# Other places in SBUF, modulo 512 bytes, for the operands of the float32r products of a two-layer hybrid transformer kernel

## The chip, the cores and the metric

One core of a Trainium2 chip runs the whole forward pass as one program. The metric is the device time of one execution in microseconds; the time before is the median of 3 runs.

## What is computed

Two layers over 256 tokens of width 2048, all in float32. Layer 0 mixes with HGRN2 (8 heads, chunked recurrence) and MLA attention (8 heads, low-rank queries and keys, rotary parts), layer 1 with retention (8 heads, keys of 256, values of 512). Behind each mixer stands a gated feed-forward part with a short causal convolution, then a gated embedding.

```python
h = x
for i in range(DEPTH):
    u = rmsnorm(h, norm_mix[i])
    h = h + (even_mixer(u, ...) if i % 2 == 0 else odd_mixer(u, ...))
    h = h + conv_ffn(rmsnorm(h, norm_ffn[i]), ffn_w_gate[i], ffn_w_up[i], ...)
    gate = jax.nn.sigmoid(rmsnorm(h, norm_ple[i]) @ ple_w_gate[i])
    h = h + (p[i] @ ple_w_proj[i]) * gate
```

Nearly all of the work is products of the 256 tokens with weight matrices; some 520 MB of weights are read once.

## The kernel before, in words

**Split products.** A float32 weight block `raw` (128 partitions by up to 1024 columns, one DMA) is split into two float32r parts: `wh`, a rounding copy by ScalarE (L158), and `wl = raw - wh` by VectorE (L161). The activations are split in the same way: a tile `xs` of 128 partitions by 512 columns holds the high part of 256 tokens in its first half and the low part in its second. A product then is high by high, high by low and low by high; low by low is left out. For each matmul TensorE loads a 128 by 128 operand (the stationary one) and streams the other past it (the moving one).

**The feature-major product** (`gemm_fm`, L172 to 199) is most of the kernel. The weights are stationary, the tile `xs` is moving. A block of 1024 weight columns makes 8 matmuls of high weights with all 512 columns of `xs` (L184). After each second block (`RUN = 2`) the low weights of both follow, with the first 256 columns of `xs` (L186). So a high run of 16 matmuls and a low run of 16 alternate; where the number of blocks is odd there are runs of 8, and with `px` of 4. The same function is used with `xs`, `hs` (the feed-forward part), `xo` (retention), `xa`, `xb` (heads of layer 0) and `px` as the moving tile. `gemm_fm1` (L201 to 215) is the same for narrower outputs: L209, L211 and L212, each with 256 columns.

**The token-major product** (`gemm_tm`, L217 to 235; `first_values`, L238 to 288, for the first matrix) turns it round: 128 columns of `xs` are stationary, 512 columns of weights are moving, in the order high by high weights (L228, L263), high by low weights (L229, L264), low by high weights (L230, L265).

**Where the tiles lie.** Tile pools lie one behind another in each partition's memory, and the tiles in a pool likewise, so each tile's size sets the start of those behind it. The sizes above are multiples of 512 bytes, so every buffer of a tag has the same start modulo 512. `LOW_SHIFT = 320` puts a pad of 320 bytes ahead of `wl`; `shift(low, "low", 64)` and `shift(l1, "l1", 64)` put 64 bytes ahead of two stage pools. As the program lays them out, before the change: `xs`, `xa`, `xb`, `hs`, `xo`, `px`, `x_kva`, `x_qa`, `raw` and `wh` begin at 64 modulo 512, `wl` at 384. In layer 1's retention the tiles `rz`, `rat` and `rv` begin at 64. Each 128-column piece of a weight tile is 512 bytes, so the piece that a matmul uses doesn't change the place modulo 512, and the same goes for the column pieces of `xs`.

**The lead.** For a matmul, call the lead the place of the next matmul's stationary operand minus the place of its own moving operand, modulo 512. Before: 0 in a high run (64 - 64), 320 in a low run (384 - 64), and in the token-major product 0, 192, 0 in turn (64 - 64, 64 - 384, 64 - 64). Retention's L1008 (`rat` stationary, `rv` moving) has 0 throughout.

**Smaller things that the change touches.** `rope_tables` loads the positions into a tile `posi` of its own and copies it to `posf` (L420 to 423). `q_rope` (L804 to 816) scales `y` (tag `ly`, two buffers) into a second tile `lyg` (L810) and rotates that: TensorE multiplies it by a permutation (L772), GpSimd multiplies it in place (L773, by the helper at L302), VectorE combines (L774, L775).

Of the kernel before, what the change touches and what calls it, by code (L numbers as in the profile page):

```python
# [8 lines left out]
F32 = mybir.dt.float32  # L9
F32R = mybir.dt.float32r  # L10
BF16 = mybir.dt.bfloat16
I32 = mybir.dt.int32
AF = mybir.ActivationFunctionType
# [4 lines left out]
P = 128  # L18
T = 256
# [5 lines left out]
F_HALVES = ((0, 24), (24, 44))  # L25
KB = 4
RUN = 2
LOW_SHIFT = 320
EPS = 1e-6

HG_HEADS = 8
# [47 lines left out]
def hybrid_kernel(ctx, tc, io):  # L79
    nc = tc.nc  # L80
# [4 lines left out]
    xpool = ctx.enter_context(tc.tile_pool(name="xpool", bufs=NX, reuse_waits="tile"))  # L85
    wpool = ctx.enter_context(tc.tile_pool(name="wpool", bufs=4))
# [18 lines left out]
    def vcol(name, i=0, n=1):  # L105
        if name == "mix0":
            return vec0[:, i:i + n]
        a = VEC[name][0] + i
        return vec[:, a:a + n]
# [7 lines left out]
    def pump():  # L117
        for g in active[:]:
            if next(g, active) is active:
                active.remove(g)  # L120
# [17 lines left out]

    shifted = set()

    def shift(pool, name, n):


        if name not in shifted:
            shifted.add(name)
            pool.tile([P, n // 4], F32, name=f"pad_{name}", bufs=1)

    def load_w(src, width):
        return split_w(fetch_w(src, width), width)

    def fetch_w(src, width):
        raw = wpool.tile([P, width], F32, tag="raw", name="raw", bufs=4)
        nc.sync.dma_start(out=raw, in_=src)
        return raw

    def split_w(raw, width):
        wh = wpool.tile([P, width], F32R, tag="wh", name="wh", bufs=3)
        nc.scalar.copy(wh, raw)  # L158
        shift(wpool, "wl", LOW_SHIFT)
        wl = wpool.tile([P, width], F32R, tag="wl", name="wl", bufs=RUN + 2)  # L160
        nc.vector.tensor_tensor(wl, raw, wh.bitcast(F32), op=ALU.subtract)  # L161
        return wh, wl

    def blocks_of(blocks, n, width, kb, sub=None):

        sub = sub or kb
        for k0 in range(0, n, sub):
            k1 = min(n, k0 + sub)
            o = (k0 % kb) * width
            yield range(k0, k1), load_w(blocks[k0 // kb][:, o:o + (k1 - k0) * width], (k1 - k0) * width)  # L170

    def gemm_fm(blocks, xs):  # L172

# [43 lines left out]
    def gemm_tm(blocks, xs, sub=None):  # L217

        ps = [psum.tile([P, 512], F32, tag="mm", name="mm", bufs=5) for _ in range(2)]
        n = len(xs)  # L220
        for ks, (wh, wl) in blocks_of(blocks, n, 512, 2, sub):
            for kc in ks:
                x = xs[kc]
                o = (kc - ks[0]) * 512
                for m in range(2):
                    xh = x[:, m * P:(m + 1) * P]
                    xl = x[:, T + m * P:T + (m + 1) * P]
                    nc.tensor.matmul(ps[m], xh, wh[:, o:o + 512], start=(kc == 0), stop=False)  # L228
                    nc.tensor.matmul(ps[m], xh, wl[:, o:o + 512], start=False, stop=False)  # L229
                    nc.tensor.matmul(ps[m], xl, wh[:, o:o + 512], start=False, stop=(kc == n - 1))  # L230
            if ks[-1] % 4 == 3:
                pump()
        return ps

    def first_values(src, xs):


        ps = [[psum.tile([P, 512], F32, tag="mm", name="mm", bufs=5) for _ in range(2)] for _ in range(2)]  # L238
        n = len(xs)
        with tc.tile_pool(name="first", bufs=4) as first:  # L240
            raws = {}

            def fetch(kc):
                if kc < 2:
                    for g in range(2):
                        raws[kc, g] = first.tile([P, 512], F32, tag="raw0", name="raw0")
                        nc.sync.dma_start(out=raws[kc, g], in_=src[kc][:, g * 512:(g + 1) * 512])
                elif kc < n:
                    raws[kc] = fetch_w(src[kc], 1024)

            def split_half(raw):
                wh = first.tile([P, 512], F32R, tag="wh0", name="wh0")
                nc.scalar.copy(wh, raw)
                wl = first.tile([P, 512], F32R, tag="wl0", name="wl0")
                nc.vector.tensor_tensor(wl, raw, wh.bitcast(F32), op=ALU.subtract)
                return wh, wl

            def products(kc, g, wh, wl, o):
                x = xs[kc]
                for m in range(2):  # L260
                    xh = x[:, m * P:(m + 1) * P]
                    xl = x[:, T + m * P:T + (m + 1) * P]
                    nc.tensor.matmul(ps[g][m], xh, wh[:, o:o + 512], start=(kc == 0), stop=False)  # L263
                    nc.tensor.matmul(ps[g][m], xh, wl[:, o:o + 512], start=False, stop=False)  # L264
                    nc.tensor.matmul(ps[g][m], xl, wh[:, o:o + 512], start=False, stop=(kc == n - 1))  # L265

            xs.fetch(0, 0)
            fetch(0)
            xs.fetch(0, 1)
            fetch(1)  # L270
            for i in range(1, 3):
                xs.fetch(i)
                fetch(2 * i)
                fetch(2 * i + 1)
            xs.fetch(3)
            for kc in range(n):
                if kc < 2:
                    for g in range(2):
                        products(kc, g, *split_half(raws[kc, g]), 0)
                else:  # L280
                    wh, wl = split_w(raws[kc], 1024)
                    for g in range(2):
                        products(kc, g, wh, wl, g * 512)
                    fetch(kc + 4)
                    if kc % 2 == 0 and kc // 2 + 3 < n // 2:
                        xs.fetch(kc // 2 + 3)
                if kc % 4 == 3:
                    pump()
        return ps
# [126 lines left out]
    rope_t = {}  # L416

    def rope_tables(tpool):
        posi = tpool.tile([P, T], I32, tag="posi", name="posi", bufs=1)
        nc.sync.dma_start(out=posi, in_=io["positions"])  # L420
        yield from steps(2)
        posf = tpool.tile([P, T], F32, tag="posf", name="posf", bufs=1)
        nc.vector.tensor_copy(posf, posi)
        for name in ("mla", "ret"):
            ang = tpool.tile([P, T], F32, tag="ang", name="ang", bufs=1)
            nc.vector.tensor_scalar(ang, posf, vcol(f"invf_{name}"), None, op0=ALU.mult)
            cs = cpool.tile([P, T], F32, name=f"cos_{name}")
            sn = cpool.tile([P, T], F32, name=f"sin_{name}")
            sin_of(sn, ang, 0.0, tpool)
            sin_of(cs, ang, 0.25, tpool)  # L430
            rope_t[name] = (cs, sn)
            yield


    def ffn_and_ple(i, st):
        rs = token_stats(st[0], D, 2)
        xs = st[1]
        cw, cb = f"cw{i}", f"cb{i}"
        st = new_norm()
        with tc.tile_pool(name=f"ffn{i}", bufs=2, reuse_waits="tile") as fp:  # L440
            silu = {}

            def gate(ps, f):
# [46 lines left out]
            xs = st[1]  # L490
# [174 lines left out]
    def even_mixer(rs, xs):  # L665
# [1 line left out]
        mix_a, mix_b = {}, {}  # L667
        first = first_values(io["w_hv"], xs)
        with tc.tile_pool(name="low", bufs=2) as low:
            shift(low, "low", 64)  # L670
            kpe = low.tile([P, 1, T], F32, name="kpe", bufs=1)
            with tc.tile_pool(name="l0a", bufs=2) as pool:
                hvs = {}
# [91 lines left out]
    def mla(pool, kpe, ckv, cq, rkv, rqa, mix, fill):  # L765
# [3 lines left out]
        def rotate(dst, y):  # L769
            ps = small([P, 2, T], "sm_rot")  # L770
            n = y.shape[1]
            nc.tensor.matmul(ps[:, 0:n], mcol("swap"), y, start=True, stop=True)  # L772
            mul(y, y, bcast(cos, n), nc.gpsimd)  # L773
            mul(dst, ps[:, 0:n], bcast(sin, n))  # L774
            nc.vector.tensor_tensor(dst, dst, y, op=ALU.add)  # L775
# [25 lines left out]
        qr, sqr, mv, pairs = {}, {}, {}, {}  # L801

        def q_rope(ps, g):
            yield from until(rqa, "bc")  # L804
            y = pool.tile([P, 2, T], F32, tag="ly", name="ly")
            mul(y, ps, bcast(rqa["bc"]))
            sq = pool.tile([P, 2, T], F32, name=f"sqr{g}", bufs=1)
            nc.scalar.activation(sq, y, AF.Square)
            yg = pool.tile([P, 2, T], F32, tag="lyg", name="lyg", bufs=1)
            nc.scalar.activation(yg, y, AF.Copy, scale=vcol("qr"))  # L810
            yield
            z = pool.tile([P, 2, T], F32, name=f"qr{g}", bufs=1)
            rotate(z, yg)
            for j in range(2):
                sqr[2 * g + j] = sq[:, j]
                qr[2 * g + j] = z[:, j]
# [111 lines left out]
    def odd_mixer(st):  # L928
        rs = token_stats(st[0], D, 2)
        xs = st[1]  # L930
        st = new_norm()
        cs, sn = rope_t["ret"]
        with tc.tile_pool(name="l1", bufs=1, reuse_waits="tile") as l1, \
                tc.tile_pool(name="l1t", bufs=2, reuse_waits="tile") as lt:
            shift(l1, "l1", 64)
            mx = {}
            rot = {}
            gates = {}
# [146 lines left out]
    xs = Arriving()  # L1085
# [120 lines left out]
```

## Time and profile before

| what | value |
|---|---|
| median of 3 runs | 2848.39 us (2848.35 to 2848.42) |
| the profiled execution's own time | 2848.95 us |
| its span, first to last instruction | 2847.1 us |
| busy: TensorE matmuls, weight loads | 2838.5 us, 2474.0 us |
| busy: VectorE, ScalarE, GpSimd | 1898.6 us, 1403.0 us, 84.7 us |
| granted TensorE clock | 1.000 of full speed |
| HBM over the span | 184 GB/s |

Read it so: matmuls are pipelined, and a matmul's recorded time (some 390 ns for 512 columns) is longer than the distance from its start to the start of the next. What the stream costs is that distance, its pace. It is read from the chain of work that ended last: a piece of that chain is a row with a start, a length and a count of matmuls, and length by count is the pace.

### The profile page before, as it was taken

To read this page: it belongs to the slowest core of one execution; us is meant where nothing else is said; L and a number is where in the kernel's file an instruction comes from. 1 tells how busy PE (TensorE), PEld (TensorE's weight loads), DVE (VectorE), ACT (ScalarE), POOL (GpSimd) and SP (SyncE) were. 2 spreads that over 40 slices of the span, in tenths; PEclk is the share of its full clock that TensorE was granted. 3 is DMA by queue.
4 is the path that set the end of the run, shared out by engine and by line. 5 is a ranking of instruction groups with operands and counts; after the bars stand their busy time and mean duration, and the time that the engine had idled before them with its cause. 6 is when DMAs were issued, how large, how long until landed. Compare 5 with 4: busy or idle time off the path is not lost.

```text
span 2847.1 us, 41083 instructions
## 1 busy us (share of the span) xinstructions
PE 2838.5 (100%) x16025; PEld 2474.0 (87%) x16025; DVE 1898.6 (67%) x2753; ACT 1403.0 (49%) x1844; POOL 84.7 (3%) x123
## 2 busy tenths in 40 slices
PE   9999999999999999999999999999999999999999
PEld 7888888888888888888888888888888888888888
DVE  8776787766557776785555555556777755777666
ACT  6665555444344444564444444445444433444444
POOL 1110300000000000000000000000000000000000
PEclk9999999999999999999999999999999999999999
DMA  7555445556655665565555555555665655666564
GB/s 242 175 157 163 133 154 189 188 191 192 192 187 191 189 189 188 187 194 183 182 180 182 189 185 181 178 178 185 196 191 186 193 189 189 192 188 194 186 194 165
DMA packets 147939, 525.58 MB, mean 185 GB/s; under 512 B 16544, under 2 KB 18336, under 8 KB 147744
## 3 DMA queue, kind: packets, MB, share of 16 engines
q1 hardware_dynamic: 147600, 522.95, 57.5%
q8 instruction: 125, 2.05, 0.3%
q14 instruction: 70, 0.57, 0.1%
q10 hardware_dynamic: 144, 0.01, 0.0%
HBM read 520.80 MB, written 2.10 MB: 184 GB/s over the span
## 4 chain that ended last, share of the span: by engine, by line
PE 98%; DVE 1%; DMA 0%; POOL 0%; issue 0%; ACT 0%; SPq 0%; DVEq 0%
PE mm L184 52%; PE mm L186 27%; PE mm L230 4%; PE mm L229 4%; PE mm L228 4%; PE sm_ro L1008 1%; PE mm L209 1%; PE mm L212 1%; PE mm L211 1%; PE mm L264 0%; PE mm L265 0%; PE sm_ra L987 0%; PE mm L263 0%; DMA raw<-in_w_hv 0%; PE sm_sc L875 0%; DVE wl L161 0%
## 5 line engine op out<-in xcount | busy, mean ns | idle before, releaser
L161 DVE TENSOR_TENSOR wl<-raw,wh 128x1024 fp32r<-128x1024 f32 (+1 forms) x990 | 1200.4, 1219 | 819.3 <-ACT wh L158 801.6
L158 ACT CAST wh<-raw 128x1024 fp32r<-128x1024 f32 (+1 forms) x990 | 1032.0, 1043 | 1205.2 <-PE mm L184 776.7
L184 PE MATMUL mm<-xs,wh 128*128 128x512 f32 x4288 | 1028.8, 391 | 0.0
L184 PEld LDWEIGHTS mm<-xs,wh 128*128 128x128 f32 x4288 | 787.1, 188 | 153.1 <-DVE xs L311 0.4
L186 PEld LDWEIGHTS mm<-xs,wl 128*128 128x128 f32 x4288 | 541.2, 189 | 19.1
L186 PE MATMUL mm<-xs,wl 128*128 128x256 f32 x4288 | 550.5, 281 | 0.0
L184 PE MATMUL mm<-hs,wh 128*128 128x512 f32 x1408 | 337.2, 391 | 0.0
L184 PEld LDWEIGHTS mm<-hs,wh 128*128 128x128 f32 x1408 | 258.2, 188 | 49.6
L229 PE MATMUL mm<-wl,xs 128*128 128x512 f32 x512 | 202.0, 394 | 0.0
L230 PE MATMUL mm<-wh,xs 128*128 128x512 f32 x512 | 201.8, 394 | 0.0
L228 PE MATMUL mm<-wh,xs 128*128 128x512 f32 x512 | 201.7, 394 | 0.0
L186 PEld LDWEIGHTS mm<-hs,wl 128*128 128x128 f32 x1408 | 179.4, 189 | 7.3
L186 PE MATMUL mm<-hs,wl 128*128 128x256 f32 x1408 | 181.7, 281 | 0.0
L295 ACT COPY evt<-mm 128x256 f32<-128x256 f32 x300 | 98.2, 374 | 92.9 <-PE mm L186 92.9
L184 PE MATMUL mm<-xo,wh 128*128 128x512 f32 x512 | 122.7, 391 | 0.0
L230 PEld LDWEIGHTS mm<-wh,xs 128*128 128x128 f32 x512 | 96.2, 188 | 22.4
L229 PEld LDWEIGHTS mm<-wl,xs 128*128 128x128 f32 x512 | 96.1, 188 | 22.1
L228 PEld LDWEIGHTS mm<-wh,xs 128*128 128x128 f32 x512 | 96.2, 188 | 21.9
L184 PEld LDWEIGHTS mm<-xo,wh 128*128 128x128 f32 x512 | 94.0, 188 | 18.5 <-DVE xo L1025 0.3
L399 DVE TENSOR_TENSOR h<-h,mm 128x256 f32<-128x256 f32 x128 | 48.1, 415 | 35.7 <-PE mm L186 35.7
L186 PEld LDWEIGHTS mm<-xo,wl 128*128 128x128 f32 x512 | 64.9, 189 | 2.4
L186 PE MATMUL mm<-xo,wl 128*128 128x256 f32 x512 | 65.9, 281 | 0.0
(275 smaller groups left out, 1952.5 us busy)
## 6 DMA issues: line engine op xcount, KB each, us to landing
raw<-in_wg SPq DMA_DIRECT2D x176, 512.0 KB, 3.7
raw<-in_wu SPq DMA_DIRECT2D x176, 512.0 KB, 4.1
raw<-in_wd SPq DMA_DIRECT2D x176, 512.0 KB, 3.9
raw<-in_w_oqk SPq DMA_DIRECT2D x64, 512.0 KB, 4.2
raw<-in_w_ov SPq DMA_DIRECT2D x64, 512.0 KB, 3.7
raw<-in_w_og SPq DMA_DIRECT2D x64, 512.0 KB, 3.5
raw<-in_w_oo SPq DMA_DIRECT2D x64, 512.0 KB, 4.1
raw<-in_wpg SPq DMA_DIRECT2D x60, 512.0 KB, 3.6
```

The costliest lines, as they stand in the source:

```text
L158: nc.scalar.copy(wh, raw)
L161: nc.vector.tensor_tensor(wl, raw, wh.bitcast(F32), op=ALU.subtract)
L184: nc.tensor.matmul(ps[j], w[:, o:o + P], xs[kc], start=(kc == 0), stop=False)
L186: nc.tensor.matmul(ps[j][:, 0:T], w[:, o:o + P], xs[kc][:, 0:T], start=False, stop=(kc == n - 1))
L209: nc.tensor.matmul(ps[:, j], w, x[:, 0:T], start=(kc == 0 and j == 0), stop=False, skip_group_check=True)
L211: nc.tensor.matmul(ps[:, j], w, x[:, T:2 * T], start=False, stop=False, skip_group_check=True)
L212: nc.tensor.matmul(ps[:, j], wl[:, o:o + P], x[:, 0:T], start=False, stop=(kc == n - 1 and j == ncol - 1), skip_group_check=True)
L228: nc.tensor.matmul(ps[m], xh, wh[:, o:o + 512], start=(kc == 0), stop=False)
L229: nc.tensor.matmul(ps[m], xh, wl[:, o:o + 512], start=False, stop=False)
L230: nc.tensor.matmul(ps[m], xl, wh[:, o:o + 512], start=False, stop=(kc == n - 1))
L295: nc.scalar.copy(tmp[:, j], ps[j][:, T:2 * T])
L399: nc.vector.tensor_tensor(h[i][:, j], h[i][:, j], ps[j][:, 0:T], op=ALU.add)
```

## The change

It moves tiles, and shares or drops two small ones to make room. The pads are now kept in one table. `xs` gets 192 bytes ahead of it and so begins at 256 modulo 512; `wh` gets 128 more and begins at 384; the buffers of `wl` are 512 bytes longer than their contents, begin at 384, and the contents stand at their start in the token-major product (384) and 192 bytes further in the feature-major one (64). The pads of the stage pools are set so that `hs`, `px`, `x_kva`, `x_qa`, `xo`, `rz`, `rat` and `rv` also begin at 256. The leads become 128 in a high run (384 - 256), 320 in a low run as before (64 - 256), and 384 throughout the token-major product (256 - 384); L1008 stays at 0. No matmul, load, copy or DMA of the products is added or left out. `posi` takes the buffer of `ang`, and `q_rope` scales `y` in place, so that `lyg` is gone.

```diff
-LOW_SHIFT = 320
+LOW_AT = {"features": 48, "tokens": 0}
+PADS = {"xs": 192, "wh": 128, "low": 256, "ret": 256, "ffn": 192}
...
-    def shift(pool, name, n):
-        if name not in shifted:
+    def shift(pool, name):
+        if name not in shifted and PADS[name[:3]]:
             shifted.add(name)
-            pool.tile([P, n // 4], F32, name=f"pad_{name}", bufs=1)
+            pool.tile([P, PADS[name[:3]] // 4], F32, name=f"pad_{name}", bufs=1)
+    shift(xpool, "xs")
...
-    def split_w(raw, width):
+    def split_w(raw, width, form):
+        shift(wpool, "wh")
         wh = wpool.tile([P, width], F32R, tag="wh", name="wh", bufs=3)
         nc.scalar.copy(wh, raw)
-        shift(wpool, "wl", LOW_SHIFT)
-        wl = wpool.tile([P, width], F32R, tag="wl", name="wl", bufs=RUN + 2)
+        wl = wpool.tile([P, 1024 + 128], F32R, tag="wl", name="wl", bufs=RUN + 2)
+        wl = wl[:, LOW_AT[form]:LOW_AT[form] + width]
         nc.vector.tensor_tensor(wl, raw, wh.bitcast(F32), op=ALU.subtract)
...
-        posi = tpool.tile([P, T], I32, tag="posi", name="posi", bufs=1)
+        posi = tpool.tile([P, T], I32, tag="ang", name="posi", bufs=1)
...
         with tc.tile_pool(name=f"ffn{i}", bufs=2, reuse_waits="tile") as fp:
+            shift(fp, f"ffn{i}")
...
-            shift(low, "low", 64)
+            shift(low, "low")
...
-            yg = pool.tile([P, 2, T], F32, tag="lyg", name="lyg", bufs=1)
-            nc.scalar.activation(yg, y, AF.Copy, scale=vcol("qr"))
+            nc.scalar.activation(y, y, AF.Copy, scale=vcol("qr"))
             yield
             z = pool.tile([P, 2, T], F32, name=f"qr{g}", bufs=1)
-            rotate(z, yg)
+            rotate(z, y)
...
-            shift(l1, "l1", 64)
+            shift(l1, "ret")
```

The rest of the diff hands `form` ("features" or "tokens") down to `split_w`; `gemm_tm` and `first_values` say "tokens".

## Rows read from the trace of the kernel before

**Rows 1.** The page: busy time, share of the span and instructions of each engine; then the chain that ended last, by engine; and from the view of that chain, its shares by line.

```profile
PE 2838.5 (100%) x16025; PEld 2474.0 (87%) x16025; DVE 1898.6 (67%) x2753; ACT 1403.0 (49%) x1844; POOL 84.7 (3%) x123
...
PE 98%; DVE 1%; DMA 0%; POOL 0%; issue 0%; ACT 0%; SPq 0%; DVEq 0%
...
by line: PE mm L184 52.2%; PE mm L186 26.9%; PE mm L230 4.3%; PE mm L229 4.3%; PE mm L228 4.3%; PE sm_ro L1008 0.6%; PE mm L209 0.6%; PE mm L212 0.5%; PE mm L211 0.5%; PE mm L264 0.4%; PE mm L265 0.4%; PE sm_ra L987 0.4%; PE mm L263 0.4%; D
```

**Rows 2.** The view of line L184, matmuls alone: moving and stationary tile, count, duration in ns (least, median, greatest), first and last start in us. L186 has the same counts.

```profile
L184 PE MATMUL mm<-xs,wh x4288: 387/389/501, 63.7 to 2827.5; 128*128 128x512 f32 x195
...
L184 PE MATMUL mm<-hs,wh x1408: 388/389/398, 696.5 to 2740.3; 128*128 128x512 f32 x176
...
L184 PE MATMUL mm<-xo,wh x512: 387/389/499, 1569.8 to 2007.3; 128*128 128x512 f32 x171
...
L184 PE MATMUL mm<-xa,wh x128: 387/393/499, 262.8 to 380.8; 128*128 128x512 f32 x128
...
L184 PE MATMUL mm<-xb,wh x128: 387/389/481, 383.2 to 427.5; 128*128 128x512 f32 x128
...
L184 PE MATMUL mm<-px,wh x64: 389/392/398, 1161.9 to 2830.3; 128*128 128x512 f32 x64
```

**Rows 3.** The view of line L228, matmuls alone, columns as in rows 2; L229 and L230 have the same counts.

```profile
L228 PE MATMUL mm<-wh,xs x512: 387/395/398, 1285.9 to 1917.0; 128*128 128x512 f32 x171
...
L228 PE MATMUL mm<-wh,x_kva x16: 387/395/398, 274.8 to 326.0; 128*128 128x512 f32 x16
```

**Rows 4.** The chain that ended last in a long stretch of token-major products (layer 1's values and gates), the first and the last of its 149 pieces of one matmul each, in the order L228, L229, L230: start in us, length in us, what.

```profile
1293.49 0.23 PE mm L230
...
1327.84 0.23 PE mm L228
```

**Rows 5.** The timeline between 449.9 and 458.3 us, where a high run ends and a low run begins: start us, length us, engine, line, what; the loads of a run and its matmuls are rows of their own.

```profile
449.68 1.29 PE L184 MATMUL mm<-xs,wh 128*128 128x512 f32 x5
...
450.59 2.06 PEld L186 LDWEIGHTS mm<-xs,wl 128*128 128x128 f32 x16
450.81 2.05 PE L186 MATMUL mm<-xs,wl 128*128 128x256 f32 x16
```

**Rows 6.** The chain that ended last between 447 and 460 us, in the gate and up products of layer 0's feed-forward part; columns as in rows 4.

```profile
447.32 3.65 PE mm L184 x16
450.97 1.89 PE mm L186 x16
452.86 3.65 PE mm L184 x16
456.51 1.89 PE mm L186 x16
```

**Rows 7.** Busy time of each engine in three stretches there, a high run, a low run and the next high run: stretch in us, its length, then busy us (instructions) of each engine, granted clock, DMA share, GB/s.

```profile
452.70:456.35 3.65, 3.65 (x18) 3.01 (x17) 2.50 (x5) 2.22 (x4) 0.00 (x0) 1.00 0.78 259
456.35:458.24 1.89, 1.89 (x18) 1.89 (x16) 1.86 (x3) 1.05 (x1) 0.00 (x0) 1.00 0.25 61
458.24:461.89 3.65, 3.65 (x18) 3.01 (x17) 1.14 (x2) 1.05 (x1) 0.00 (x0) 1.00 0.77 259
```

**Rows 8.** The chain that ended last between 1331 and 1345 us, in layer 1's retention, columns as in rows 4.

```profile
1333.83 2.04 PE sm_ro L1008 x9
1335.87 1.81 PE mm L184 x8
1337.68 1.89 PE mm L186 x16
1339.57 3.66 PE mm L184 x16
```

**Rows 9.** The same view between 1163 and 1176 us, at the start of layer 0's embedding.

```profile
1167.12 0.58 PE mm L184 x2
1167.69 1.82 PE mm L186 x16
1169.52 1.84 PE mm L184 x8
```

**Rows 10.** The lines of TensorE's matmuls by form in a part of the high run of rows 7 that begins at 452.70 us (452.95 to 453.55), and further on in it (453.90 to 456.1): count, then busy us and mean ns of one.

```profile
L184 PE MATMUL mm<-xs,wh 128*128 128x512 f32 x4 | 1.1, 394 | 0.0
...
L184 PE MATMUL mm<-xs,wh 128*128 128x512 f32 x11 | 2.7, 389 | 0.0
```

**Rows 11.** The same view in a low run of rows 6 and 7 (456.35 to 458.2), and in the low run of rows 9 (1167.9 to 1169.3).

```profile
L186 PE MATMUL mm<-xs,wl 128*128 128x256 f32 x16 | 2.0, 281 | 0.0
...
L186 PE MATMUL mm<-xs,wl 128*128 128x256 f32 x15 | 1.9, 276 | 0.0
```

**Rows 12.** The chain that ended last, between 1163 and 1176 us and between 1331 and 1345 us: matmuls of 1 column (L361) and of 128 columns (L1022), each with a load of 128 by 128 float32.

```profile
1166.66 0.46 PE sm_col L361 x4
...
1343.22 0.87 PE sm_rt L1022 x8
```

**Rows 13.** The view of the tile lyg: first its instructions (durations in ns: least, median, greatest; first and last start in us), then what waited for it (us, times); and from the view of the tile ly, its second product's first reader.

```profile
L810 ACT ACTIVATE lyg<-ly,vec x2: 709/716/722, 285.2 to 290.6; 128x512 f32<-128x512 f32 x2
L302 POOL TENSOR_TENSOR lyg<-lyg,cos_mla x2: 1296/1692/2087, 287.5 to 292.5; 128x512 f32<-128x512 f32 x2
L775 DVE TENSOR_TENSOR qr<-qr,lyg x2: 679/1220/1760, 289.8 to 294.7; 128x512 f32<-128x512 f32 x2
...
  PE sm_rot L772: 0.6, 1
...
L830 ACT ACTIVATE sq<-ly x4: 626/632/641, 292.1 to 351.3; 128x512 f32<-128x512 f32 x4
L848 ACT ACTIVATE sq<-ly x4: 613/630/632, 297.0 to 357.4; 128x512 f32<-128x512 f32 x4
```

More of the change, by code (lines that the diff above doesn't have):

```diff
@@ L139, in hybrid_kernel, with load_w @@
     shifted = set()
-    def shift(pool, name, n):
-        if name not in shifted:
+    def shift(pool, name):
+        if name not in shifted and PADS[name[:3]]:
             shifted.add(name)
-            pool.tile([P, n // 4], F32, name=f"pad_{name}", bufs=1)
-    def load_w(src, width):
-        return split_w(fetch_w(src, width), width)
+            pool.tile([P, PADS[name[:3]] // 4], F32, name=f"pad_{name}", bufs=1)
+    shift(xpool, "xs")
+    def load_w(src, width, form):
+        return split_w(fetch_w(src, width), width, form)
     def fetch_w(src, width):
@@ L154, in fetch_w, with blocks_of @@
         return raw
-    def split_w(raw, width):
+    def split_w(raw, width, form):
+        shift(wpool, "wh")
         wh = wpool.tile([P, width], F32R, tag="wh", name="wh", bufs=3)
         nc.scalar.copy(wh, raw)
-        shift(wpool, "wl", LOW_SHIFT)
-        wl = wpool.tile([P, width], F32R, tag="wl", name="wl", bufs=RUN + 2)
+        wl = wpool.tile([P, 1024 + 128], F32R, tag="wl", name="wl", bufs=RUN + 2)
+        wl = wl[:, LOW_AT[form]:LOW_AT[form] + width]
         nc.vector.tensor_tensor(wl, raw, wh.bitcast(F32), op=ALU.subtract)
         return wh, wl
-    def blocks_of(blocks, n, width, kb, sub=None):
+    def blocks_of(blocks, n, width, kb, sub=None, form="features"):
         sub = sub or kb
@@ L169, in blocks_of @@
             o = (k0 % kb) * width
-            yield range(k0, k1), load_w(blocks[k0 // kb][:, o:o + (k1 - k0) * width], (k1 - k0) * width)
+            yield range(k0, k1), load_w(
+                blocks[k0 // kb][:, o:o + (k1 - k0) * width], (k1 - k0) * width, form)
     def gemm_fm(blocks, xs):
@@ L220, in gemm_tm @@
         n = len(xs)
-        for ks, (wh, wl) in blocks_of(blocks, n, 512, 2, sub):
+        for ks, (wh, wl) in blocks_of(blocks, n, 512, 2, sub, "tokens"):
             for kc in ks:
@@ L280, in first_values @@
                 else:
-                    wh, wl = split_w(raws[kc], 1024)
+                    wh, wl = split_w(raws[kc], 1024, "tokens")
                     for g in range(2):
```

## The prediction

> **What bounds the kernel now.** First the page's busy times and its chain: TensorE holds 98% of the chain, the products alone (L184, L186, L228 to L230) 92%, and VectorE, ScalarE and the DMAs next to nothing [rows 1]. Waiting is not where time can be won; the reader has to look at the pace of back-to-back matmuls. Counts come next: 4288 + 1408 + 512 + 128 + 128 + 64 = 6528 high matmuls and as many low ones [rows 2], and 3 x 528 = 1584 token-major ones [rows 3], to which the first matrix adds 192 by its code. Then the paces, length by count. Token-major: (1327.84 - 1293.49) / 148 = 232.1 ns [rows 4].
>
> For the feature-major runs the reader should compare equal work in different places. Loads run beside the matmul before: the first load of a low run begins at 450.59, its matmul at 450.81, 0.22 us later, one high matmul's pace [rows 5]. In the steady alternation a high run of 16 takes 3.65 us and a low one 1.89, or 228.1 and 118.1 ns each [rows 6]. It is not the other engines' doing: two high runs take 3.65 with VectorE busy for 2.50 and 1.14 us of them, at a granted clock of 1.00 throughout [rows 7]. But behind L1008, whose lead is 0 too, eight high matmuls take 1.81 us, 226.3 ns each, and L1008 itself 2.04 / 9 = 226.7; entered from a low run, eight take 1.84 [rows 8, 9]. So a high run loses some 0.03 us on entering, and this falls into its first matmuls: 394 ns of duration there, 389 later [rows 10]. Low runs have two paces as well: entered from a settled high run 1.89 us, entered from a two-matmul remnant of one behind an interruption 1.82 us, 113.8 ns each, with durations of 281 and 276 [rows 8, 9, 11]. Same instructions, same places, other history: a state is handed on from matmul to matmul, and at some of its values the matmul runs slower. I take that state to be the time by which the running load is ahead of or behind the stream, and the slow values to be those where both read the same place modulo 512. That is theory; the two paces are rows.
>
> **The change, part by part.** The sum is made against the profiled execution's 2848.95 us (span 2847.1), 0.56 us above the median.
>
> *High runs, lead 0 to 128.* Settled high matmuls (226.7) are the quickest rows of their kind, so only the entering loss can go: 3.65 - 16 x 0.2267 = 0.023 us by one pair of rows, 1.84 - 1.81 = 0.03 by the other; I take 0.025 [rows 6, 8, 9]. 6528 matmuls make 408 runs of 16 or, with some runs of 8, about 430: 10.8 us in all. Why it should go: a load of 512 bytes per partition takes at most 0.46 / 4 = 115 or 0.87 / 8 = 109 ns where loads follow each other [rows 12], so 128 bytes are 27 to 29 ns of load, just what a high run loses until it has settled. If each slow matmul pushes the stream later until the two readers are apart, weights that lie 128 bytes further on are apart from the start. Bounds: loss gone, -12.9 us (430 x 0.03); loss doubled, because the push would have to be the other way, +12.9. I take -10.8, since the size fits.
>
> *Low runs, lead 320 as before.* Their own places relative to each other don't change; what changes is the state in which they are entered, by the same 27 ns. The low run that loses 0.07 us comes from a settled high run; the one that doesn't comes from a state short of settled [rows 9]. If high and low runs rest in one state, the low pace goes from 118.1 to 113.8 ns: 4.3 x 6528 = 28.1 us. I take 8 in 10 of it, 22.5, because runs behind waits and in the 8-matmul stages start anew. Bounds: none of it, 0; all, -28.1; a worse state, of which no row tells, would be at most as bad again, +28.1.
>
> *Token-major, leads 0, 192, 0 to a constant 384.* L1008, also of 512 columns but with one constant lead, runs at 226.7; these run at 232.1 and never settle over 149 matmuls [rows 4, 8]. With one lead they should settle: 5.4 x 1776 = 9.6 us; I take 8, for each stretch has to settle first. Bounds: -9.6; staying as now, 0; each stuck in a slow place like the 394 ns matmuls, 5 ns over settled, so again about 0.
>
> *The rest.* The narrow products (480 matmuls) share the leads of high and low runs; I give them -1. The place of `posi` costs nothing: its reader and the next writer of that buffer are both VectorE. `q_rope`: the same ScalarE product of 709 to 722 ns, written in place, behind the square that reads `y` on the same engine, so TensorE's 0.6 us of waiting there stays [rows 13]. `y` is now held until VectorE's sum, whose last start is 294.7; the next users of these buffers have their first readers at 292.1 and 297.0, and their writer is VectorE, in order, so its order covers it. If it doesn't, one wait on GpSimd's product, up to 2.1 us [rows 13]. Copies and DMAs at other places: VectorE works 4.36 us in the 5.54 us of a high and a low run, ScalarE 3.27 [rows 7], and would stay clear of the bound if the pair shrank to 5.45.
>
> Sum: -10.8 - 22.5 - 8 - 1 = -42.3; 2848.95 - 42.3 = 2806.65, and against the median 2806.
>
> **A rule against it.** The Trainium skill, "TensorE: Matmul & The Clock Gate", section "Step-by-step: what each phase is for", says that TensorE has two independent read ports into SBUF, one for the stream and one for the load, and that loading the next tile's weights takes no read bandwidth from the running matmul. By that rule places cannot matter, and the time would stay at 2848. The two paces of equal runs in rows 8 and 9 speak for some coupling of load and stream, but no row here moves a place for the same run.
>
> **Rivals.**
>
> *Only part of it (2829).* High runs lose their entry and token-major settles, but low runs keep 118 ns, because whatever they are entered with, they fall into the slow state: 2848.4 - 10.8 - 8 - 1 = 2829. For it: nearly all low runs behind settled high runs are slow, and their own lead stays.
>
> *No change (2848).* The states come from something that doesn't hang on places, such as the order of loads; or the edits trade gains (token-major -8, high entry +11). For it: the settled high pace is the same with leads 0 in two unlike products.
>
> *Slower (2872).* One mechanism: a lead of 128 is a place where the load and the stream meet in the middle of each load, and the high runs never settle, as the token-major stream with its changing leads never does. Price: from 228.1 to the token-major 232.1 is 4.0 x 6528 = 26 us; with nothing else 2874, with 2 us of token-major gain 2872. It decides from 2.1 ns per high matmul on: 2.1 x 6528 = 13.7 eats 8 us of token-major and exceeds it by 5.7. For it: only leads of 0, 192 and 320 have rows, and at 0 the high runs do settle, so the change gives up a place known to be quiet.
>
> **How the numbers follow.** About 0.2% (5.7 us) is what a measurement tells from no change. Chances: forecast 0.42 (2796 to 2814: all losses gone gives 2848.4 - 12.9 - 28.1 - 9.6 - 2 = 2796), part 0.25 (2814 to 2842), no change 0.18 (2843 to 2854), slower 0.15 (2854 to 2876). Faster is 0.42 + 0.25 = 0.67, same 0.18, slower 0.15. The range takes in the first three, 0.85 in all, from 2795 to 2853.
>
> **What would show it.** Right: high runs of 16 at 3.63 us or less right behind low runs, low runs of 16 at 1.82, a token-major pace near 227 ns; TensorE still about 98% of the chain, counts unchanged. The part case shows 3.63 beside 1.89; the slower one high runs of 3.70 and more with durations of 394 in all their matmuls. Wrong altogether: gains or losses on waits of TensorE, or VectorE and ScalarE copies that grow and enter the chain.

## The result and the profile after

The changed kernel takes 2860.77 us in the median of 6 runs (2860.3 to 2862.43) against 2848.48 us before (6 runs), a ratio of 1.0043 with a 95% interval of 1.0033 to 1.0053: slower by 12.3 us, where 42 less were forecast. Its profiled execution has a span of 2858.5 us.

The page after: busy times, the chain by engine, and the chain's shares by line. Six lines were added further up: high runs are L190 now (L184 before), low runs L192 (L186), the token-major product L234 to L236 (L228 to L230), retention's product L1014 (L1008).

```profile
PE 2851.2 (100%) x16025; PEld 2464.8 (86%) x16025; DVE 1899.0 (66%) x2753; ACT 1401.5 (49%) x1844; POOL 84.7 (3%) x123
...
PE 98%; DVE 1%; DMA 0%; issue 0%; POOL 0%; SPq 0%; ACT 0%; DVEq 0%
...
by line: PE mm L190 53.0%; PE mm L192 26.4%; PE mm L235 4.3%; PE mm L236 4.3%; PE mm L234 4.2%; PE mm L215 0.6%; PE mm L218 0.6%; PE mm L217 0.6%; PE sm_ro L1014 0.6%; PE mm L270 0.4%; PE mm L271 0.4%; PE sm_ra L993 0.4%; PE mm L269 0.4%; D
```

Counts are those of [rows 1], TensorE still has 98% of the chain, and VectorE and ScalarE are as busy as before. The time is again in the pace of back-to-back matmuls: L190's share rose from 52.2 to 53.0%, L192's fell from 26.9 to 26.4%. The chain that ended last in the stretch of [rows 6] (start us, length us, what):

```profile
447.19 3.72 PE mm L190 x16
450.91 1.82 PE mm L192 x16
452.73 3.71 PE mm L190 x16
456.44 1.89 PE mm L192 x16
```

Every high run is longer by 0.06 to 0.07 us, and every second low run shorter by 0.07. Two pairs take 3.72 + 1.82 + 3.71 + 1.89 = 11.14 us where two of before take 2 x 5.54 = 11.08, so 0.03 a pair, and 6528 / 16 = 408 pairs make 12.2 us: as much as the whole result. Summing the distances from each matmul's start to the next over the whole trace, wherever the waits lie, gives 12.3 for the three kinds of product below; the two spans differ by 11.4, for the rest of the program is 0.9 shorter in the trace after.

| product (matmuls) | before, us | after, us | difference |
|---|---|---|---|
| high (6528) | 1495.4 | 1519.6 | +24.2 |
| low (6528) | 771.8 | 759.3 | -12.5 |
| token-major with the first matrix (1776) | 414.9 | 415.5 | +0.6 |

Why the high runs are longer is read from the durations. Of the high run whose row begins at 452.73 us, all 16 matmuls, and of the next one its last 11 (by form: count, busy us, mean ns of one):

```profile
L190 PE MATMUL mm<-xs,wh 128*128 128x512 f32 x16 | 3.9, 394 | 0.0
...
L190 PE MATMUL mm<-xs,wh 128*128 128x512 f32 x11 | 2.7, 396 | 0.0
```

Before, 394 ns was the duration on entering and 389 the settled one [rows 10]. After the change the high runs never settle. Nor does the token-major stream with its constant lead; the first and the last of 140 pieces of the chain, one matmul each:

```profile
1297.55 0.23 PE mm L236
...
1329.98 0.23 PE mm L234
```

(1329.98 - 1297.55) / 139 = 233.3 ns, where [rows 4] gave 232.1. And retention's product, whose lead is 0 before and after, lost its settled pace too (chain that ended last):

```profile
1336.28 1.86 PE mm L190 x8
1338.14 2.09 PE sm_ro L1014 x9
1340.24 1.86 PE mm L190 x8
```

Nine matmuls take 2.09 us, 232 ns each, against 2.04 in [rows 8]. That row speaks against leads: the lead is the same, only the places moved from 64 to 256. It is the first thing that the experiments had to settle.

### The profile page after: what moved, and what is told of

Same layout as the page of the kernel before. It is cut to its first block, busy times and chain, and to the rows that moved or that the text cites. A ratio compares the mean times of both kernels' runs of the same rounds, so it can differ in the third digit from the quotient of the medians.

```text
span 2858.5 us, 41084 instructions
## 1 busy us (share of the span) xinstructions
PE 2851.2 (100%) x16025; PEld 2464.8 (86%) x16025; DVE 1899.0 (66%) x2753; ACT 1401.5 (49%) x1844; POOL 84.7 (3%) x123
## 4 chain that ended last, share of the span: by engine, by line
PE 98%; DVE 1%; DMA 0%; issue 0%; POOL 0%; SPq 0%; ACT 0%; DVEq 0%
PE mm L190 53%; PE mm L192 26%; PE mm L235 4%; PE mm L236 4%; PE mm L234 4%; PE mm L215 1%; PE mm L218 1%; PE mm L217 1%; PE sm_ro L1014 1%; PE mm L270 0%; PE mm L271 0%; PE sm_ra L993 0%; PE mm L269 0%; DVE wl L166 0%; PE sm_sc L881 0%; PE sm_rt L1028 0%
## 5 line engine op out<-in xcount | busy, mean ns | idle before, releaser
L190 PE MATMUL mm<-xs,wh 128*128 128x512 f32 x4288 | 1045.1, 395 | 0.0
L190 PEld LDWEIGHTS mm<-xs,wh 128*128 128x128 f32 x4288 | 788.2, 188 | 164.9 <-DVE xs L317 0.4
L192 PEld LDWEIGHTS mm<-xs,wl 128*128 128x128 f32 x4288 | 534.1, 188 | 21.8
L192 PE MATMUL mm<-xs,wl 128*128 128x256 f32 x4288 | 542.1, 279 | 0.0
L190 PE MATMUL mm<-hs,wh 128*128 128x512 f32 x1408 | 342.6, 394 | 0.0
L190 PEld LDWEIGHTS mm<-hs,wh 128*128 128x128 f32 x1408 | 258.5, 188 | 53.4
L234 PE MATMUL mm<-wh,xs 128*128 128x512 f32 x512 | 202.1, 395 | 0.0
L236 PE MATMUL mm<-wh,xs 128*128 128x512 f32 x512 | 202.1, 395 | 0.0
L192 PEld LDWEIGHTS mm<-hs,wl 128*128 128x128 f32 x1408 | 176.8, 188 | 8.4
L192 PE MATMUL mm<-hs,wl 128*128 128x256 f32 x1408 | 178.6, 279 | 0.0
L190 PE MATMUL mm<-xo,wh 128*128 128x512 f32 x512 | 124.6, 395 | 0.0
L236 PEld LDWEIGHTS mm<-wh,xs 128*128 128x128 f32 x512 | 96.4, 188 | 22.4
L234 PEld LDWEIGHTS mm<-wh,xs 128*128 128x128 f32 x512 | 96.4, 188 | 22.0
L190 PEld LDWEIGHTS mm<-xo,wh 128*128 128x128 f32 x512 | 94.1, 188 | 19.9 <-DVE xo L1031 0.3
L192 PEld LDWEIGHTS mm<-xo,wl 128*128 128x128 f32 x512 | 64.0, 188 | 2.8
L192 PE MATMUL mm<-xo,wl 128*128 128x256 f32 x512 | 64.9, 279 | 0.0
```

Of the source, the lines that this page charges most:

```text
L190: nc.tensor.matmul(ps[j], w[:, o:o + P], xs[kc], start=(kc == 0), stop=False)
L192: nc.tensor.matmul(ps[j][:, 0:T], w[:, o:o + P], xs[kc][:, 0:T], start=False, stop=(kc == n - 1))
```

## The experiments

Theory A: the pace depends on the lead alone, not on the places. Theory B: the places count by themselves. Theory C: other engines or DMAs make the loss.

### The map: one stream at each place

Edit: a kernel of its own that leaves the model out, with loops like this, over 8 by 8 places:

```python
for i in range(32):
    nc.tensor.matmul(ps[i % 2], stationary(i, s), moving(i // 2, m, 512), start=(i < 2), stop=(i >= 30))
```

> A kernel that measures the disputed cost by itself: the reference's products are left out, and its output means nothing. From one arena that begins at 0 modulo 512 it streams 32 matmuls of 512 columns for each of 8 x 8 places of the moving and the stationary operand in steps of 64 bytes, and then token-major triples (24 matmuls) for x tiles at 64 and 256 and 8 x 8 places of the high and the low weights. No other engine and no DMA works beside it. Theory A (only the lead counts): the settled pace is the same along each line of equal lead, 226.7 ns at lead 0 and about 232.2 at 128, as in the runs of before and after. Theory B (places count by themselves): moving 64 and stationary 64 gives 226.7, as before, and 256 with 256 some 232, as L1008's counterpart (L1014) has after the change. Theory C (other engines' traffic makes the loss): all 64 pairs give 226.7 here. Of the triples A expects one pace for each pair of leads, 232 at (x 64, weights 64 and 384) and 233 at (256, 384, 384).

Measured: mean distance of starts from the 13th to the 32nd matmul of each stream, over eight moving places. The very first stream is left out: its first distances are 427 ns, although the granted clock of that stretch reads 1.00.

| lead, bytes | 0 | 64 | 128 | 192 | 256 | 320 | 384 | 448 |
|---|---|---|---|---|---|---|---|---|
| mean, ns | 226.7 | 233.5 | 232.5 | 228.9 | 226.7 | 233.5 | 232.5 | 228.9 |
| greatest minus least over the places | 0.1 | 0.1 | 0.7 | 0.3 | 0.1 | 0.1 | 0.7 | 0.4 |

The lines by form of three of these streams, moving and stationary at 64 and 64 (lead 0), 256 and 256 (lead 0), and 64 and 128 (lead 64):

```profile
L49 PE MATMUL acc<-arena 128*128 128x512 f32 x18 | 4.2, 389 | 0.0
...
L49 PE MATMUL acc<-arena 128*128 128x512 f32 x18 | 4.2, 389 | 0.0
...
L49 PE MATMUL acc<-arena 128*128 128x512 f32 x17 | 4.1, 395 | 0.0
```

B and C fall: place 256 settles at lead 0 like place 64, and the loss is there with no other engine at work. A stands, with a correction: the period is 256 bytes, not 512.

L1014's loss is then left to come from the state in which it is entered. Three of the runs below bear on that: the two of the cross, first with the leads of before at place 256, then with the changed leads at place 64, and at last the feature-major part alone, at place 256 again (there the line is L1016):

```profile
1330.08 1.84 PE mm L190 x8
1331.92 2.04 PE sm_ro L1014 x9
...
1335.61 1.86 PE mm L190 x8
1337.47 2.09 PE sm_ro L1014 x9
...
1335.11 1.86 PE mm L192 x8
1336.97 2.05 PE sm_ro L1016 x9
```

The loss is there at place 64 and gone at place 256, so it isn't one of the places. Nor are unsettled high runs ahead of it enough: in the last run they take 1.86 us for eight as after the change, and L1016 settles all the same. There the token-major product further ahead is settled, which it isn't after the change. What exactly is handed on to it isn't shown.

Of the token-major triples (mean from the 6th matmul of each on) the pair of leads (0, 192) of before gives 231.9 ns, the changed (384, 384) 232.7, and only both leads at 0 or 256 give 226.6 to 227.8. One lead for all three is not enough; it has to be this one.

### The map of runs in turn

Edit: in the same kernel, 16 matmuls of 512 columns and 16 of 256 in turn, three times for each pair of leads.

> The same kind of kernel, with the reference's products left out: high runs of 16 matmuls with 512 columns and low runs of 16 with 256 in turn, three times for each of 8 x 8 places of the high and the low weights, with the moving tile at 64 and then at 256. The pair takes 3.65 + 1.89 = 5.54 us before and 3.715 + 1.855 = 5.57 after. Theory A (leads): the table for 256 is that for 64 moved by 192 in both weights' places, with 5.54 at leads (0, 320) and 5.57 at (128, 320); and somewhere in it a pair near 3.63 + 1.82 = 5.45, where both settle. Theory B (places by themselves): the two tables don't match when moved. Theory C (other engines): all entries alike.

Measured, in the chain that ended last: leads 0 and 320 with the moving tile at 64, then at 256; and leads 128 and 320 with it at 64, then at 256 (L55 the high runs, L58 the low ones).

```profile
250.72 3.65 PE acc L55 x16
254.37 1.89 PE acc L58 x16
...
1643.26 3.65 PE acc L55 x16
1646.91 1.89 PE acc L58 x16
...
517.77 1.89 PE acc L58 x16
519.65 3.72 PE acc L55 x16
523.37 1.82 PE acc L58 x16
525.20 3.71 PE acc L55 x16
...
1905.85 3.72 PE acc L55 x16
1909.58 1.83 PE acc L58 x16
1911.40 3.71 PE acc L55 x16
1915.12 1.89 PE acc L58 x16
```

These are the runs of the kernels before and after to a hundredth of a microsecond, the turn of 1.82 and 1.89 included, without any of the kernels' other work. The hoped-for pair of 3.63 + 1.82 is nowhere in the table: over its second and third rounds the pairs take 5.49 to 5.64 us. The two tables differ in a few entries, all at a high lead of 128 or 192 (modulo 256), by up to 0.04 us a pair. All of these stand among the first three behind a change of the high lead in one of the tables, where another stream had gone before, so the history is the likely cause and not the place; no run tests that by itself.

### Leads of before at the new places

```diff
-LOW_AT = {"features": 48, "tokens": 0}
-PADS = {"xs": 192, "wh": 128, "low": 256, "ret": 256, "ffn": 192}
+LOW_AT = {"features": 80, "tokens": 80}
+PADS = {"xs": 192, "wh": 0, "low": 384, "ret": 384, "ffn": 320}
```

> The changed kernel with the leads of before at the new places: x tiles, hs, xo and px at 256, high weights at 256, low weights at 64 in both products, so that the leads are 0, 320 and in the token-major product 0, 192, 0. Theory A (leads): the time of before, 2848 within 3 us, high runs of 16 at 3.65 us. Theory B (places by themselves): high runs unsettled as after the change, 3.71 and more, about 2860 or above.

Measured: 2847.19 us, ratio 0.9996 to the kernel before (0.9987 to 1.0006). The chain that ended last:

```profile
450.92 3.65 PE mm L190 x16
454.57 1.89 PE mm L192 x16
```

As A says. All of the change's other edits are in this run (pads, `posi`, `lyg`, longer `wl` buffers), so they cost nothing that can be measured.

### Leads of the changed kernel at the places of before

```diff
-PADS = {"xs": 192, "wh": 128, "low": 256, "ret": 256, "ffn": 192}
+PADS = {"xs": 0, "wh": 128, "low": 256, "ret": 256, "ffn": 192}
```

> The other half of that cross: the leads of the changed kernel (128, 320, 384) at the places of before, with x tiles, hs, xo and px at 64, high weights at 192, low weights at 384 (feature-major) and 192 (token-major). Theory A (leads): the time of after, 2861 within 3 us, high runs of 16 at 3.71 to 3.72. Theory B (places by themselves, x tiles at 64 being what lets high runs settle): high runs at 3.65 or less, about 2848 or below.

Measured: 2860.41 us, ratio 1.0042 (1.0027 to 1.0057), the time of after.

```profile
450.45 1.82 PE mm L192 x16
452.27 3.71 PE mm L190 x16
455.98 1.89 PE mm L192 x16
457.87 3.72 PE mm L190 x16
```

With the run before, the cross is closed: the time goes with the leads, whatever the places.

### Finer steps and shorter loads

Edit: in the kernel of the map, leads in steps of 16 bytes, and `stationary(i, s)[:, 0:cols]` with 32 and 64 columns.

> A measuring kernel like the first, the reference's products left out, moving tile at 64. Since the map of 64-byte steps came out with a period of 256 bytes in the lead, this one takes leads from 0 to 240 in steps of 16 bytes, for 512 columns (32 matmuls each) and for 256 columns (48 each); then 512 columns past stationary operands of 32 and of 64 columns only; then high and low runs of 16 in turn, four times for each pair of leads in steps of 32 bytes. Theory A (lead modulo 256): values between 226.7 (lead 0) and the 233.5, 232.5 and 228.9 of leads 64, 128 and 192, with 240 perhaps as settled as 0; some pair of leads takes under 5.54 us. Theory D (what counts is only whether load and stream stand at the same place modulo 64 bytes or less): the steps inside 64 bytes show a pattern of their own. If the load causes even the 13 ns that the settled pace has over 512 columns at 2.4 GHz (213.3), operands of 32 columns run at less than 226.7; if the stream causes it, they run at 226.7 as well, and none of the leads matters to them as much.

Measured, as above: with 512 columns, 226.6 ns at leads 16 and 240, next to the 0 of the first map, and 230.1 to 233.9 at all others; the 192 that gave 228.9 in the first map gave 233.3 here, entered from another stream. With 256 columns alone the order is another one: 113.3 ns at leads 64 and 192, 120.0 at 0, 116.6 to 120.0 elsewhere. Past operands of 32 columns the stream runs at 231 to 240 ns at every lead, past 64 columns at 226.7 to 232.5. The loads themselves are shorter, by form 189 ns for 128 columns, 135 for 64 and 108 for 32 (count, busy us, mean ns of one):

```profile
L49 PEld LDWEIGHTS acc<-arena 128*128 128x128 f32 x1280 | 188.4, 189 | 31.9 <-ACT arena L30 8.8
L72 PEld LDWEIGHTS acc<-arena 128*64 128x64 f32 x256 | 34.4, 135 | 24.5
L72 PEld LDWEIGHTS acc<-arena 128*32 128x32 f32 x256 | 27.7, 108 | 31.6
```

So a shorter load doesn't make the stream quicker, and neither of the two outcomes that were expected for 32 columns came (less than 226.7, or 226.7 with leads that matter less). With 512 columns nothing was seen settled below 226.6, and theory D finds no pattern that repeats every 64 bytes. The best pair of runs in turn is high and low lead both 192: 3.66 and 3.68 with 1.88 and 1.81, 5.51 us over the last three rounds.

### Token-major lead 0

```diff
-LOW_AT = {"features": 80, "tokens": 80}
+LOW_AT = {"features": 80, "tokens": 0}
```

(against the run with all leads of before)

> The places of the run with all leads of before at 256, but the low weights of the token-major product at 256 too, so that all its leads are 0 (high runs 0, low runs 320 as before). Theory A: token-major matmuls go from 232.0 to 227 to 228 ns as in the map, 1776 x 4.5 = 8 us less: about 2839 to 2840, faster than before. Theory B (a constant lead is enough to settle, whatever it is): the same time, but then the changed kernel's 384 would have settled too. If token-major stays near 232, as other work beside it would make it, the time stays at 2847.

Measured: 2839.47 us, ratio 0.9968 (0.9956 to 0.9980). The first and the last of 166 pieces of the chain, one matmul each:

```profile
1291.98 0.23 PE mm L236
...
1329.38 0.23 PE mm L236
```

(1329.38 - 1291.98) / 165 = 226.7 ns. This is the gain that the prediction had put on the change, 8 us, got with the lead that the change didn't choose.

### All leads moved by 256

```diff
-PADS = {"xs": 192, "wh": 0, "low": 384, "ret": 384, "ffn": 320}
+PADS = {"xs": 192, "wh": 256, "low": 128, "ret": 128, "ffn": 64}
```

(against the run above)

> The run with the token-major leads at 0, but with every lead moved by 256: high runs 256, low runs 64, token-major 256 and 0 in turn by 256 (x tiles at 256, high weights at 0, low weights at 64 in the feature-major product and at 0 in the token-major one). Theory A with a period of 256 bytes: the same time, 2839.5 within 2 us, high runs of 16 at 3.65, low ones at 1.89. Theory A with a period of 512: these are leads of which the runs of whole kernels tell nothing, and the time would move by more than 5 us one way or the other.

The low weights of the feature-major product lie at 320 in this run, not at 64 as written above; their lead is 64, as stated there. Measured: 2839.8 us, ratio 0.9968 (0.9956 to 0.9980), with these runs of matmuls:

```profile
451.81 3.65 PE mm L190 x16
455.47 1.89 PE mm L192 x16
```

The period of 256 holds in the whole kernel.

### The feature-major part alone

Edit (against the token-major lead 0): `wh` and `wl` buffers 256 bytes longer than their contents, which are shifted by form; pads set anew. Buffers of one tag then lie 0 or 256 apart modulo 512, so the leads hold modulo 256.

```diff
+HIGH_AT = {"features": 32, "tokens": 0}
+LOW_AT = {"features": 16, "tokens": 0}
...
-        wh = wpool.tile([P, width], F32R, tag="wh", name="wh", bufs=3)
+        wh = wpool.tile([P, 1024 + 64], F32R, tag="wh", name="wh", bufs=3)
+        wh = wh[:, HIGH_AT[form]:HIGH_AT[form] + width]
```

> The feature-major part of the change alone: high runs at lead 128, low runs at 320 (modulo 256: 64), as changed, but the token-major leads at 0. Theory A, parts add up: 12.3 us above the run that differs in the high lead alone (2839.5), so 2852, with high runs of 3.71 to 3.72 us and low ones of 1.82 and 1.89 in turn. If the changed token-major stream or the stage pools had part in the loss, less than 2852.

Measured: 2851.61 us, ratio 1.001 (1.0001 to 1.0020), 12.1 us above the token-major lead 0 and 9.2 below the changed kernel.

```profile
447.13 3.72 PE mm L192 x16
450.86 1.82 PE mm L194 x16
452.68 3.71 PE mm L192 x16
456.39 1.89 PE mm L194 x16
```

(L192 are the high runs here, L194 the low ones.) The parts add up: high lead 128 costs 12, token-major lead 0 is worth 8 to 9.

### A version that beats both

As the last, with `{"features": 48, "tokens": 0}` for both parts: high and low lead 192, token-major 0.

> Token-major leads 0, and high and low runs both at lead 192 (modulo 256), for which the measuring kernel shows high runs of 3.66 and 3.68 us in turn and low runs of 1.88 and 1.81 in turn, 5.516 for a pair where leads 0 and 320 take 5.540. Theory A: 408 pairs x 0.024 = 10 us less than the run with the token-major leads at 0, about 2830. If runs of whole kernels are entered in other states than there (blocks of 8, interruptions, waits), between 2822 and 2842.

Measured: 2832.2 us, ratio 0.9941 to the kernel before (0.9927 to 0.9956).

```profile
450.48 3.68 PE mm L191 x16
454.16 1.81 PE mm L193 x16
455.98 3.66 PE mm L191 x16
459.63 1.88 PE mm L193 x16
```

The turn of the measuring kernel is there (L191 high, L193 low): against leads 0 and 320 the high runs lose 0.02 us a pair, and the low runs gain 0.045. The gain on the run with the token-major leads at 0 is 7.3 us, where 10 were expected. It wasn't sure beforehand that the kernel would fall into this turn: in the first map of runs in turn, of three rounds each, the same leads gave 5.52 us a pair over the last two rounds in one entry and 5.55 in the others.

## Why the prediction was wrong, step by step

**What bounds the kernel** held: TensorE's pace is the time, before and after, and no wait took part in the loss.

**High runs** are where it failed, forecast -10.8 us, measured +24.2. The failing step reads: "If each slow matmul pushes the stream later until the two readers are apart, weights that lie 128 bytes further on are apart from the start." It rested on one coincidence (27 ns of load, 23 to 30 ns of loss), and it took for granted that a high run settles at any lead. The map shows that it doesn't: at lead 128 the distances go round between 228 and 241 ns, every seven or eight matmuls, at a mean of 232.5 for as long as the stream lasts, and a stream settles at 226.6 or 226.7 only at leads 0 and 256 and 16 bytes beside them. The bound of +12.9 was wrong for the same reason, since it priced a longer entry, not a run that never settles.

**The slower rival** had the mechanism: "a lead of 128 is a place where the load and the stream meet in the middle of each load, and the high runs never settle". Its price, 26 us, came out as 24.2, its time of 2872 was too high by 11 because it left the low runs alone. That the two meet in the middle is still only argued. It had been given 0.15, and its own reason, that the change gives up the one place known to be quiet, was better evidence than the coincidence; the range's upper end of 2853 left it out.

**Low runs**, forecast -22.5, measured -12.5: the reasoning by entry was right in kind, and the sign was luck in part. Their lead didn't change, and they did gain, but by being entered from unsettled high runs, where the forecast had put high runs that settle at once; and only every second one gained. What differs can be read ahead of them: the last matmul of the high run before the quick low run of 450.91 us, and of the one before the slow low run of 456.44 (columns as above):

```profile
L190 PE MATMUL mm<-xs,wh 128*128 128x512 f32 x1 | 0.4, 398 | 0.0
...
L190 PE MATMUL mm<-xs,wh 128*128 128x512 f32 x1 | 0.4, 392 | 0.0
```

It holds throughout the trace after. Where a full high run goes ahead of a full low run and another high run follows, the distance from the last high matmul to the first low one is 229 or 230 ns ahead of all 168 slow low runs (1.89 us) and 233 to 236 ns ahead of all 169 quick ones (1.82 or 1.83). Before the change it is 225 or 226 in all 337 cases, and all are slow. So a quick low run goes with a high run that is cut off at a slow point of its round. That is a regularity of the traces; no run sets this distance by itself.

**Token-major**, forecast -8, measured +0.6: the step "With one lead they should settle" mistook the reason why L1008 settles. It is lead 0, not the constancy. With lead 0 the stream ran at 226.7 ns and gained 8.

**The rest** was forecast at -1 for the narrow products and at nothing otherwise. The narrow products took 0.6 us less, and the other edits cost nothing that the runs resolve: the run with all leads of before has these edits and the time of before.

**The rule** of two independent read ports ("TensorE: Matmul & The Clock Gate", "Step-by-step: what each phase is for", in the Trainium skill) would have given 2848, as the prediction read it for places. The trace disagrees: the leads alone moved the high matmuls by 24.2 us, and the map moves a stream from 226.7 to 233.5 ns with TensorE at work alone. Whether read bandwidth is what the two share, no run here shows.

**Still open**: what the state is that is handed on, of which the last distance of a high run is only a sign, and why 0 is quiet for 512 columns and 64 and 192 for 256 alone. In all these streams the matmul's own operand and the next one lie at the same place, so the runs don't tell which of the two loads counts.

## What to carry to other kernels

Where back-to-back matmuls set the time, the place of the stationary operand against the moving one is worth a map: a small kernel that streams a few dozen matmuls at each pair of places gives in one run what rows of the big kernel can only hint at, and here it matched the big kernel's runs to 0.01 us. A settled place that rows show is evidence; a better one that is argued from one matching number isn't, and giving up the first for the second needs the map first. Where two kinds of runs alternate, map them in turn, since each enters the other in the state that it leaves.

## What the runs showed of the hardware

- In streams of 32 float32r matmuls of 512 columns at one lead, the pace depends on the lead with a period of 256 bytes: 226.7 ns at 0, 228.9 to 233.3 at 192, 232.5 to 233.6 at 128, 233.2 to 233.5 at 64, at a granted clock of 1.00.
- It does so with the other engines idle and 1 GB/s of DMA, and not by the place: eight moving places agree within 0.8 ns.
- The same stream can run at different paces by its history: 228.9 and 233.3 ns at lead 192, and 1.82 and 1.89 us for the same low run of 16 at lead 320.
- In the trace after, a low run is quick in 169 of 169 cases where the high matmul ahead of it stands 233 to 236 ns before it, and slow in 168 of 168 where it stands 229 or 230.
- Halving or quartering the stationary columns did not shorten the pace; with 64 columns its mean was 226.7 to 232.5 ns, with 32 it was 230.9 to 239.9.
